# Ranking one head by itself, loading three U blocks with the query weights, and fetching late rows two ahead instead of four

## The chip, the cores and the metric

The kernel runs on one core of a Trainium2 chip. The metric is the device time of one execution in microseconds. Times are given for the whole program: the trunk layer with its caches and states, and the expert stage behind it.

## The reference

One inference step of one layer: 272 prompt rows (16 learned tokens and 256 new ones) and 8 × 8 rows of running sequences, 336 tokens of width 1024. The trunk (convolution branch, state-space branch, gates, output projection) is not touched by the change. Behind it stands a mixer that picks experts by product keys:

```python
q = (xb @ w_q).reshape(T, PEER_HEADS, 2, D_KEY // 2)
s = jnp.einsum('thcd,hckd->thck', q, keys).astype(jnp.float32)
s1, i1 = lax.top_k(s[:, :, 0], PEER_TOPK)
s2, i2 = lax.top_k(s[:, :, 1], PEER_TOPK)
cand = (s1[..., :, None] + s2[..., None, :]).reshape(T, PEER_HEADS, PEER_TOPK * PEER_TOPK)
sc, f = lax.top_k(cand, PEER_TOPK)
ids = (jnp.take_along_axis(i1, f // PEER_TOPK, axis=-1) * N_KEYS
       + jnp.take_along_axis(i2, f % PEER_TOPK, axis=-1))
g = jax.nn.softmax(sc, axis=-1)
act = jax.nn.gelu(jnp.einsum('thkd,td->thk', U[ids], xb).astype(jnp.float32), approximate=False)
w = (g * act).astype(xb.dtype)
return jnp.einsum('thk,thkd->td', w, V[ids])
```

There are 8 heads, 128 × 128 = 16384 experts with a row of U and a row of V each (1024 floats), and 16 experts for each token and head. Both outputs of the tokens are normalised behind it.

## The kernel before

Of the 320 tokens that reach the expert stage, 128 and another 16 are served by **gathering**: their chosen rows of U and V are fetched from memory. The other 176 are served **densely**: all U and V are streamed through TensorE (PE) and the unwanted experts are multiplied by zero.

**Queries and ranks.** Sixteen query projections (two per head; L1097 to L1113) are computed in program order. Each loads a block of weights (`weight`, L241: a load on SP into one of four raw buffers, a high part cast on ScalarE (ACT), a low part subtracted on GpSimd (POOL) or VectorE (DVE), two buffers each), makes 24 matmuls, copies the query to SBUF on ACT and multiplies it by the keys (psc, L1105). The scores are copied on ACT, for the gathered tokens into `sco` (9 buffers), for the dense ones into `sall`. `top16` (L995) finds the 16 best of 128 with five VectorE operations. `heads` (L1053) then ranks four heads of the gathered tokens: the sums of pairs, their 16 best, the table look-up of the ids, the ids in `gid`, and the softmax weights in `ggw`. It is called behind projections 7 and 15. The rank tasks of the dense tokens (`topk_tasks`, L1124) come later in program order; those of projections above 5 are ordered behind the first write of `gid`.

**Fetches.** A column is the n-th expert of all 128 gathered tokens, so one fetch (L1083) is an indirect DMA on POOL's queue of 128 rows of 8 KB, 1 MB, into one of five buffers `wuv` (one of which first holds a row of norm weights). There are 144: columns 0 to 63, 16 for the 16 extra tokens, 64 to 127. `ahead(n)` (L1092) gives out fetches up to n + 3. It is called once behind projection 7 and then by every `pick_row`. From the 93rd U block on, a fetch waits for the block matmul that lies `LEAD` = 4 blocks before the newest one in program order. `pick_row(n)` (L1212) is a dot product on VectorE (L1195), two small steps on ACT (L1197, L1198), and the weighted sum of V on VectorE (L1203).

**Dense blocks.** U and V have 128 blocks each of 512 KB, loaded on SP into a ring of eight buffers that served the weights before (`ring`, L1257). `u_block` (L1267) makes 16 matmuls into one of six PSUM buffers, and ACT writes the Gelu into S (L1274). S lies where the inputs of the query projections lay. `g_step` (L1280) multiplies S by the softmax weights of the chosen experts; its short matmuls `pg` (L1301) are ordered behind U or V blocks. `v_block` (L1363) makes 16 matmuls into standing sums. The transposes `pix` (L1163) that bring the dense ranks to PE are ordered behind U blocks 38 and 50.

**Order.** The program order interleaves tasks: `Feed` (L1239) spreads the rank tasks and 44 pick rows over the first 88 U blocks, 30 pick rows and half of the G steps over the other 40, 42 pick rows and the other half over the first 64 V blocks, and the last 29 of 145 rows over the rest. A scheduler then orders each engine's instructions from this program order, by its own estimate of the times; each engine works through its list in that order. Where `add_manual_dep` is used with `NoSync` only this order is bound.

The constants that matter: `HG` = 4 heads a call, `UV` = 5 buffers, `SB` = 88, `HB` = 64, `LASTP` = 126.

## Time and profile before

| | |
|---|---|
| runs | 1375.5, 1370.0, 1370.71 us; median 1370.71 |
| profiled execution | 1375.22 us, of which the span is 1373.5 |
| granted TensorE clock, mean | 0.983 |
| moved in all | 382.05 MB, mean 278 GB/s |
| fetches | queue q0: 20736 packets, 151.00 MB |
| loads and stores of SP | queue q1: 65056 packets, 227.46 MB |

The page is read from its slices: each stands for a fortieth of the span, 34.3 us. The trunk fills slices 0 to 15, the queries 16 and 17, the U blocks 18 to 28, the V blocks 29 to 39. Busy time, clock and transfer rate then show which stage is limited by what. An engine's idle time matters only where the chain of work that ends last passes through it; of that chain PE has 77%, DVE 12% and the transfers 8% of the span. The lines that carry this stand in the prediction.

### The profile page before, as it was taken

What the parts mean: (1) busy time and instruction counts of PE and PEld (TensorE: products, weight loads), DVE (VectorE), ACT (ScalarE), POOL (GpSimd) and SP (SyncE); (2) the same over time, 40 slices, a digit from 0 to 9 for tenths busy, and PEclk for the clock granted to TensorE, in tenths of its full rate; (3) what the DMA queues carried; (4) which work ended last, traced back from release to release, by engine and by line L of the source; (5) the groups of instructions that cost most, each with busy time, mean ns of one, the idle gap of its engine ahead of it and who ended that gap; (6) DMA issues with size and microseconds to landing.
All of it is one profiled execution on the core that took longest, in us unless ns stands there. A gap on an engine that the chain in (4) does not pass through costs nothing.

```text
span 1373.5 us, 24602 instructions
## 1 busy us (share of the span) xinstructions
PE 1319.4 (96%) x9324; PEld 1250.6 (91%) x9324; DVE 1017.6 (74%) x2340; ACT 526.4 (38%) x1393; POOL 581.7 (42%) x492
## 2 busy tenths in 40 slices
PE   9999999999999999998999988999999999987997
PEld 7888888888889999898998988999999999976897
DVE  7898777887866346799999885668787777766543
ACT  6777777777666434442222121111111111111101
POOL 2477776786746667542212331123222212344110
PEclk9999999999999999999999998999999999999999
DMA  6445545445344445439999999899999999999993
GB/s 237 160 127 171 166 160 162 142 149 187 108 142 127 150 154 165 148 114 380 398 413 393 409 416 362 288 416 363 372 416 415 380 377 390 395 417 416 414 412 113
DMA packets 87094, 382.05 MB, mean 278 GB/s; under 512 B 10144, under 2 KB 15648, under 8 KB 66368
## 3 DMA queue, kind: packets, MB, share of 16 engines
q1 hardware_dynamic: 65056, 227.46, 45.7%
q0 software_dynamic: 20736, 151.00, 27.3%
q10 hardware_dynamic: 1184, 2.02, 0.4%
q8 instruction: 73, 1.20, 0.3%
q14 instruction: 45, 0.37, 0.1%
HBM read 367.41 MB, written 13.03 MB: 277 GB/s over the span
## 4 chain that ended last, share of the span: by engine, by line
PE 77%; DVE 12%; DMA 8%; ACT 2%; issue 1%; POOL 0%; ACTq 0%; DVEq 0%
PE pj L150 30%; PE va L1366 19%; PE pj L1272 16%; DMA eraw<-in_vE_dram 5%; PE pg L1301 4%; PE pst L150 2%; DMA eraw<-in_uT_dram 2%; DVE wuv L1195 1%; DVE ygat L1203 1%; PE po L150 1%; PE py L150 1%; DVE pcv L473 1%; PE pdec L150 1%; PE ptr L155 1%; PE psc L1105 1%
## 5 line engine op out<-in xcount | busy, mean ns | idle before, releaser
L1083 POOL DMA_INDIRECT wuv<-in_peer_uv_dram,gid x144 | 183.0, 1271 | 523.4 <-DVE ygat L1203 159.7
L1272 PE MATMUL pj<-nd,eraw 128*128 128x176 f32 x2048 | 325.4, 320 | 11.5 <-DMA eraw<-in_uT_dram 7.6
L1366 PE MATMUL va<-S,eraw 128*128 128x176 f32 x2048 | 318.0, 315 | 18.9 <-DMA eraw<-in_vE_dram 18.9
L218 POOL TENSOR_TENSOR wl<-wraw,wh 128x1024 fp32r<-128x1024 f32 x111 | 267.2, 2408 | 149.7 <-ACT wh L217 78.0
L1366 PEld LDWEIGHTS va<-S,eraw 128*128 128x128 f32 x2048 | 307.6, 191 | 24.4 <-DMA eraw<-in_vE_dram 22.1
L1272 PEld LDWEIGHTS pj<-nd,eraw 128*128 128x128 f32 x2048 | 314.8, 195 | 13.5 <-ACT S L1274 8.8
L150 PE MATMUL pj<-ah,wh 128*128 128x336 f32 (+1 forms) x768 | 243.8, 329 | 0.7 <-ACT xnf L193 0.7
L150 PE MATMUL pj<-al,wh 128*128 128x336 f32 (+1 forms) x768 | 233.8, 318 | 0.0
L1203 DVE SCALAR_TENSOR_TENSOR ygat<-wuv,scg,ygat 128x1024 f32<-128x1024 f32 x128 | 163.9, 1280 | 57.8 <-ACT scg L1198 56.5
L1197 ACT ACTIVATE scg<-scg 128x1 f32<-128x1 f32 x144 | 29.0, 202 | 418.1 <-DVE wuv L1195 412.8
L1195 DVE SCALAR_TENSOR_TENSOR wuv<-wuv,x2m 128x1024 f32<-128x1024 f32 x128 | 156.0, 1218 | 42.6 <-DMA wuv<-in_peer_uv_dram,gid 42.6
L217 ACT CAST wh<-wraw 128x1024 fp32r<-128x1024 f32 x125 | 131.2, 1050 | 117.1 <-PE pj L150 79.9
L473 DVE SCALAR_TENSOR_TENSOR pcv<-ccat,vec,pcv 128x256 f32<-128x256 f32 x464 | 148.8, 379 | 17.1 <-ACT pcv L471 17.1
L150 PEld LDWEIGHTS pj<-ah,wh 128*128 128x128 f32 x768 | 147.1, 192 | 8.6 <-ACT xnf L193 2.7
L150 PEld LDWEIGHTS pj<-al,wh 128*128 128x128 f32 x768 | 146.5, 192 | 0.7
L150 PE MATMUL pj<-ah,wl 128*128 128x336 f32 (+1 forms) x768 | 137.0, 315 | 0.0
L150 PEld LDWEIGHTS pj<-ah,wl 128*128 128x128 f32 x768 | 120.5, 188 | 0.8 <-issue 0.7
L1274 ACT ACTIVATE S<-pj 128x176 f32<-128x176 f32 x128 | 37.6, 312 | 157.3 <-PE pj L1272 155.2
L1301 PE MATMUL pg<-oh 128*128 128x64 bf16 x1056 | 74.9, 242 | 0.0
L1308 DVE TENSOR_TENSOR S<-S,pg 128x192 f32<-128x192 f32 (+1 forms) x66 | 31.6, 506 | 56.9 <-PE pg L1301 56.9
L1301 PEld LDWEIGHTS <-oh 128*128 128x128 bf16 x1056 | 70.9, 117 | 2.2
L487 DVE SCALAR_TENSOR_TENSOR pj<-mcat,vec,pj 128x360 f32<-128x360 f32 x96 | 56.3, 588 | 3.6 <-ACT pj L485 3.6
(366 smaller groups left out, 1703.4 us busy)
## 6 DMA issues: line engine op xcount, KB each, us to landing
eraw<-in_uT_dram SPq DMA_DIRECT2D x128, 512.0 KB
eraw<-in_vE_dram SPq DMA_DIRECT2D x128, 512.0 KB
wraw<-in_w_in_dram SPq DMA_DIRECT2D x80, 512.0 KB
st<-in_state_dram SPq DMA_DIRECT2D x8, 1024.0 KB
out_ssm_s_dram<-st SPq DMA_DIRECT2D x8, 1024.0 KB
wraw<-in_w_mo_dram SPq DMA_DIRECT2D x16, 512.0 KB
wraw<-in_w_q_dram SPq DMA_DIRECT2D x16, 512.0 KB
wraw<-in_w_co_dram SPq DMA_DIRECT2D x8, 512.0 KB
```

Source lines behind the costliest of these rows:

```text
L150: i_ = nc.tensor.matmul(*a_, **kw)
L217: (nc.vector.tensor_copy if on_dve else nc.scalar.copy)(h, src)
L218: (nc.gpsimd if on_pool else nc.vector).tensor_tensor(l, src, h.bitcast(F32), op=OP.subtract)
L473: t = nc.vector.scalar_tensor_tensor(o, i_, wv, a_, op0=OP.mult, op1=OP.add)
L487: nc.vector.scalar_tensor_tensor(o, cat[:, w:w + n], wv, o, op0=OP.mult, op1=OP.add)
L1083: i_ = nc.gpsimd.indirect_dma_start(out=u, out_offset=None, in_=ia["peer_uv"], in_offset=bass.IndirectOffsetOnAxis(ap=gid[:, c:c + 1], axi ...
L1195: nc.vector.scalar_tensor_tensor(u[:, :D], u[:, :D], 1.0, x2m if c < NPICK else x2e, op0=OP.mult, op1=OP.mult, accum_out=w)
L1203: nc.vector.scalar_tensor_tensor(a_, u[:, D:], scg[:, c:c + 1], a_, op0=OP.mult, op1=OP.add)
L1272: i_ = nc.tensor.matmul(p[:, :ND], raw[:, k, :], nd[:, k, :], start=(k == 0), stop=(k == KD - 1))
L1274: nc.scalar.activation(Sv(b), p[:, :ND], AF.Gelu)
L1301: i_ = nc.tensor.matmul(pg[:, q, :], B[:, q // 4, :, q % 4], A[:, c_, q // 4, :, q % 4], start=(c_ == 0), stop=(c_ == 2))
L1366: i_ = nc.tensor.matmul(va[k // 2][:, k % 2], raw[:, k, :], Sv(b), start=False, stop=(b == 127), skip_group_check=True)
```

## The change

`heads` gets the number of heads as an argument. It is called for head 0 behind projection 1, for heads 1 to 3 behind projection 7, and for heads 4 to 7 behind projection 15. The first call of `ahead` stays behind projection 7 in program order, and fetches need only the ids of their own column. `ahead` gives out four fetches as before while at most 64 V blocks have been given out, and two afterwards (`DEEP`, `NEAR`).

Behind projection 6, U blocks 0 to 2 are loaded into a tile of their own (`pre`, 12 KB per partition). Their matmuls are taken out of `u_block` into `u_mm`, stand behind the sixteen projections in program order, and are ordered on PE behind the first score matmul of projection 12 (`PREJ`). `u_block` then only takes their Gelu. All other blocks are loaded and multiplied as before.

```diff
--- before.py
+++ after.py
@@ -43,6 +43,10 @@
 NCOL = NPICK + (NPICK // XQ if NX else 0)
 XAT = 64
 HG = 4
+BATCH = ((0, 1), (1, 3), (4, 4))
+NPRE = 3
+PREJ = 12
+FETCH = 7
 LEAD = 4
 GT = 8
 SB = 88
@@ -55,6 +59,8 @@
 RB = 4
 OH = 2
 UV = 5
+DEEP = 4
+NEAR = 2
 GLAG = 14
 PLACE = (38, 50)
 LASTP = 126
@@ -1050,28 +1056,28 @@
 
         early = []
 
-        def heads(h0):
-            hs_ = slice(h0, h0 + HG)
-            cs = slice(16 * h0, 16 * (h0 + HG))
-            sf = table(128, HG, si[0][:, 2 * h0:2 * h0 + 2 * HG])
-            c, cf = candidates(128, HG, sv[0].rearrange("p (h c) k -> p h c k", c=2)[:, hs_])
-            for h in range(HG):
+        def heads(h0, n_):
+            hs_ = slice(h0, h0 + n_)
+            cs = slice(16 * h0, 16 * (h0 + n_))
+            sf = table(128, n_, si[0][:, 2 * h0:2 * h0 + 2 * n_])
+            c, cf = candidates(128, n_, sv[0].rearrange("p (h c) k -> p h c k", c=2)[:, hs_])
+            for h in range(n_):
                 top16(cv0, ci0, cf[:, h], h0 + h)
-            ab = places(128, HG, ci0.rearrange("p h k -> p (h k)")[:, cs])
-            pk = kp.tile([128, 2, HG * 16], F32, name="pkh")
+            ab = places(128, n_, ci0.rearrange("p h k -> p (h k)")[:, cs])
+            pk = kp.tile([128, 2, HG * 16], F32, name="pkh")[:, :, :n_ * 16]
             for half in range(2):
-                look(pk[:, half], 128, HG, ab[half], sf, half, c)
-            idf = kp.tile([128, HG * 16], F32, name="idh")
+                look(pk[:, half], 128, n_, ab[half], sf, half, c)
+            idf = kp.tile([128, HG * 16], F32, name="idh")[:, :n_ * 16]
             nc.vector.scalar_tensor_tensor(idf, pk[:, 0], float(NK), pk[:, 1], op0=OP.mult, op1=OP.add)
             early.append(nc.vector.tensor_copy(gid[:, cs], idf).ins.name)
-            g_ = kp.tile([128, HG, 16], F32, name="gh")
-            nc.vector.tensor_tensor(g_, cv0[:, hs_], cv0[:, hs_, 0:1].to_broadcast([128, HG, 16]), op=OP.subtract)
+            g_ = kp.tile([128, HG, 16], F32, name="gh")[:, :n_]
+            nc.vector.tensor_tensor(g_, cv0[:, hs_], cv0[:, hs_, 0:1].to_broadcast([128, n_, 16]), op=OP.subtract)
             act(g_, g_, AF.Exp, scale=rsT[:, 0:1])
-            sm = kp.tile([128, HG], F32, name="smh")
+            sm = kp.tile([128, HG], F32, name="smh")[:, :n_]
             nc.vector.tensor_reduce(sm, g_, axis=AX.X, op=OP.add)
             nc.vector.reciprocal(sm, sm)
             nc.vector.tensor_tensor(ggw[:, cs].rearrange("p (h k) -> p h k", k=16), g_,
-                                    sm[:, :, None].to_broadcast([128, HG, 16]), op=OP.mult)
+                                    sm[:, :, None].to_broadcast([128, n_, 16]), op=OP.mult)
 
         COLS = list(range(XAT)) + list(range(NPICK, NCOL)) + list(range(XAT, NPICK))
         pend = {}
@@ -1090,10 +1096,26 @@
             return u
 
         def ahead(n):
-            for i_ in range(n, min(n + UV - 1, NCOL)):
+            for i_ in range(n, min(n + (DEEP if len(vstep) <= HB else NEAR), NCOL)):
                 if i_ not in pend:
                     pend[i_] = gather(COLS[i_])
 
+        def u_mm(b, raw):
+            tag, nb = (("pj", 3), ("y", 2), ("pj", 3), ("y", 2), ("pj", 3), ("pb", 1))[b % 6]
+            p = ps.tile([128, PJ], F32, name="pj", tag=tag, bufs=nb)[:, :T]
+            for k in range(KD):
+                i_ = nc.tensor.matmul(p[:, :ND], raw[:, k, :], nd[:, k, :], start=(k == 0), stop=(k == KD - 1))
+                if k == 0 and b < NPRE:
+                    tc.add_manual_dep(i_.ins, scored[PREJ], mybir.DependencyInfo(mybir.DependencyClass.NoSync,
+                                                                                 mybir.DependencyReason.DATA),
+                                      reason="behind the scores")
+            ustep.append(i_.ins.name)
+            return p
+
+        scored = []
+
+        us = ExitStack()
+        up = us.enter_context(tc.tile_pool(name="up", bufs=1))
         for j in range(16):
             w = weight(ia["w_q"], j)
             p = pj()
@@ -1102,15 +1124,24 @@
             nc.scalar.copy(qT[:, :T2], p[:, :T2])
             p = misc([128, 3, NK], "psc")
             for i, (t0, L) in enumerate(KTILES):
-                nc.tensor.matmul(p[:L, i], qT[:, t0:t0 + L], keys[:, j, :], start=True, stop=True)
+                i_ = nc.tensor.matmul(p[:L, i], qT[:, t0:t0 + L], keys[:, j, :], start=True, stop=True)
+                if i == 0:
+                    scored.append(i_.ins.name)
                 s_ = sall[:, i - 1, j] if i else kp.tile([128, NK], F32, name="sco", bufs=9)
                 nc.scalar.copy(s_[:L], p[:L, i])
                 if i == 0:
                     top16(sv[i], si[i], s_[:L], j)
-            if j % (2 * HG) == 2 * HG - 1:
-                heads(j // 2 - HG + 1)
-            if j == 2 * HG - 1:
+            for h0, n in BATCH:
+                if j == 2 * (h0 + n) - 1:
+                    heads(h0, n)
+            if j == FETCH:
                 ahead(0)
+            if j == 6:
+                pre = up.tile([128, NPRE, D], F32, name="pre")
+                for b in range(NPRE):
+                    nc.sync.dma_start(pre[:, b], ia["uT"][b])
+        early_u = [u_mm(b, pre[:, b].rearrange("p (k m) -> p k m", k=KD)) for b in range(NPRE)]
+        us.close()
         qs.close()
         xs.close()
         s0p = top.enter_context(tc.tile_pool(name="s0p", bufs=1, side=RIGHT))
@@ -1265,12 +1296,7 @@
             return raw.rearrange("p (k m) -> p k m", k=KD)
 
         def u_block(b):
-            raw = block(ia["uT"], b)
-            tag, nb = (("pj", 3), ("y", 2), ("pj", 3), ("y", 2), ("pj", 3), ("pb", 1))[b % 6]
-            p = ps.tile([128, PJ], F32, name="pj", tag=tag, bufs=nb)[:, :T]
-            for k in range(KD):
-                i_ = nc.tensor.matmul(p[:, :ND], raw[:, k, :], nd[:, k, :], start=(k == 0), stop=(k == KD - 1))
-            ustep.append(i_.ins.name)
+            p = early_u[b] if b < NPRE else u_mm(b, block(ia["uT"], b))
             nc.scalar.activation(Sv(b), p[:, :ND], AF.Gelu)
 
         def after(i_, name):
```

## The prediction

> **What bounds the kernel now.** The page comes first: its head, the engines, the forty slices.
>
> ```profile
> span 1373.5 us, 24602 instructions
> PE 1319.4 (96%) x9324; PEld 1250.6 (91%) x9324; DVE 1017.6 (74%) x2340; ACT 526.4 (38%) x1393; POOL 581.7 (42%) x492
> DMA  6445545445344445439999999899999999999993
> GB/s 237 160 127 171 166 160 162 142 149 187 108 142 127 150 154 165 148 114 380 398 413 393 409 416 362 288 416 363 372 416 415 380 377 390 395 417 416 414 412 113
> ```
>
> The matrix engine is busy nearly everywhere, and from slice 18 (about 620 us) the transfers run at some 415 GB/s too. So two resources are near their limits in the expert stage, which the change touches. The view of busy time by windows shows where PE falls behind. Columns: window, length, busy time (count) of PE, PEld, DVE, ACT, POOL; clock, DMA share, GB/s.
>
> ```profile
> 600.00:620.00 20.00, 20.00 (x134) 18.52 (x134) 19.57 (x90) 8.07 (x23) 9.57 (x4) 1.00 0.45 146
> 645.00:763.00 118.00, 113.52 (x725) 112.62 (x726) 117.19 (x389) 30.28 (x98) 28.92 (x23) 0.96 1.00 401
> 763.00:805.00 42.00, 42.00 (x296) 41.90 (x297) 34.16 (x51) 9.65 (x43) 16.18 (x12) 1.00 1.02 412
> 805.00:840.00 35.00, 27.41 (x194) 26.50 (x193) 21.33 (x34) 4.83 (x21) 7.26 (x6) 0.85 1.02 415
> 840.00:994.00 154.00, 154.00 (x1277) 153.01 (x1276) 113.68 (x179) 28.05 (x106) 34.76 (x27) 1.00 0.94 354
> 994.00:1193.00 199.00, 199.00 (x1626) 196.40 (x1625) 153.19 (x249) 22.06 (x86) 44.45 (x41) 1.00 1.00 395
> 1204.00:1282.00 78.00, 59.13 (x357) 54.45 (x356) 51.16 (x61) 9.95 (x40) 31.00 (x18) 0.98 1.02 416
> 1282.00:1345.00 63.00, 63.00 (x424) 63.00 (x424) 25.18 (x30) 4.97 (x20) 9.37 (x8) 1.00 1.01 406
> ```
>
> In 1282 to 1345 PE does 424 matmuls in 63 us, 6.73 per us, 2.38 us per block of 16: full speed. At that rate the 357 of 1204 to 1282 are 53 us of work, so **25 us are lost** there; the 725 of 645 to 763 are 108, so 10 are lost. For 805 to 840 the short G matmuls must be kept apart, with the same view of the U line alone:
>
> ```profile
> 800.00:840.00 40.00, 27.97 (x150) 26.47 (x151) 0.87 1.02 415
> 805.39 1.65 PE L1301 MATMUL pg<-oh 128*128 128x64 bf16 x24
> 806.86 5.03 PE L1272 MATMUL pj<-nd,eraw 128*128 128x176 f32 x32
> ```
>
> 150 U matmuls are 22.3 us; the three G groups in between (24 matmuls, 1.47 us from one start to the next) 4.4. So **13 us are lost** in 800 to 840. What ends both stalls is a block that has not landed, because row fetches take the bandwidth:
>
> ```profile
> 833.41 5.03 PE L1272 MATMUL pj<-nd,eraw 128*128 128x176 f32 x16 [3.91 <-DMA eraw<-in_uT_dram]
> 1228.25 2.65 PE L1366 MATMUL va<-S,eraw 128*128 128x176 f32 x16 [1.10 <-DMA eraw<-in_vE_dram]
> 1232.02 2.65 PE L1366 MATMUL va<-S,eraw 128*128 128x176 f32 x16 [1.12 <-DMA eraw<-in_vE_dram]
> q0 software_dynamic: 2283, 16.63, 67.1%
> q1 hardware_dynamic: 2286, 8.32, 34.4%
> ```
>
> The two q rows are the DMA view of 1205 to 1265. Packets are equal, bytes are two to one for the fetches, and a V block comes every 3.77 us (1228.25 to 1232.02), not every 2.38. The fetches come in bursts; POOL's windows for the fetch line alone (length, busy, count):
>
> ```profile
> 600.00:763.00 163.00, 34.76 (x29) 0.97 0.93 366
> 763.00:830.00 67.00, 23.02 (x18) 0.97 1.02 414
> 1193.00:1264.00 71.00, 33.12 (x21) 0.98 1.02 417
> 1264.00:1322.00 58.00, 11.81 (x11) 1.00 1.02 415
> ```
>
> Spacing is 3.7 us in 763 to 830, 3.4 in 1193 to 1264, above 5 in the other two: each burst has a stall in it. The first exists because until 763 VectorE is full of ranking; afterwards only picks are left in its order.
>
> **Part 1: head 0 alone, fetches and U blocks early.** The first ids exist when the cast to gid runs:
>
> ```profile
> 574.94 0.27 ACT L1107 COPY sco<-psc 128x128 f32<-128x128 f32 x1 [0.56 <-PE psc L1105]
> L1066 DVE CAST gid<-idh x2: 184/186/188, 622.5 to 693.7; 128x64 int32<-128x64 f32 x2
> 622.92 1.15 POOL L1083 DMA_INDIRECT wuv<-in_peer_uv_dram,gid  x1 [6.67 <-DVE sv L997]
> 632.86 1.21 DVE L1195 SCALAR_TENSOR_TENSOR wuv<-wuv,x2m 128x1024 f32<-128x1024 f32 x1
> 580.00:600.00 20.00, 17.39 (x115) 1.00 0.29 88
> 566.00:580.00 14.00, 7.96 (x36) 0.76 0.29 94
> ```
>
> (The last two are windows of VectorE.) Head 0 needs scores 0 and 1; the second is copied at 575, and VectorE still has idle time then, so its ids can exist near 590 to 600 and the first pick near 610 rather than 632.9: 20 us earlier, at some 5 us a pick four picks. Four fetches of 1.05 MB and three U blocks of 0.52 MB are 5.8 MB, 14 us of transfer at 415 GB/s, moved to a time when the engines are 0.29 to 0.45 busy. That is not the gain: in 645 to 763 VectorE is 117.19 of 118 us busy, so picks done earlier push ranking later. The gain is a shorter burst. With four of 18 picks gone, at about 3.8 us each while transfers limit, it ends 15 us sooner, of the 25 between 805 and 830; 60% of 13 us is 8. I take **7 us**, bounds 0 (VectorE hands out no pick earlier) and 13.
>
> The U blocks by themselves: 48 matmuls move between projections 13 to 15, but PE is 20.00 of 20 busy there, so nothing is saved; ahead of 645 six blocks can be computed in either order, for the six PSUM buffers. They are ordered behind score 12, and behind them on PE stand the last projections; their loads are some 40 us old by then, so PE waits for none. Three load issues move on SP ahead of the weights of projections 7 to 15, which have four raw buffers; bandwidth is free, so 0.
>
> The gap that follows:
>
> ```profile
> 644.24 0.44 PE L1105 MATMUL psc<-keys,qT 128*64 128x128 f32 x2 [2.72 <-ACT sall L1107]
> 643.50 0.20 ACT L1197 ACTIVATE scg<-scg 128x1 f32<-128x1 f32 x1 [2.53 <-DVE wuv L1195]
> 644.00:648.00 4.00, 2.76 (x9) 2.76 (x10) 0.57 1.01 417
> ```
>
> A score copy stood behind a pick's Gelu in ACT's order; PE ran dry and its clock fell to 0.57. Moved picks may dissolve this or put the same hold, and ACT's table changes between Exp and Gelu, elsewhere: bounds −10 (all of 645 to 763) and +10, taken **−2**.
>
> Cost: ranking in three calls, not two, adds 26 VectorE instructions (one table, two candidate sums, five places, twelve look-ups, six for ids and softmax). At 0.19 us (the cast's row) that is 5 us, against 8.7 idle in 566 to 600. Some meet POOL's low-part subtractions:
>
> ```profile
> L1073 DVE TENSOR_TENSOR ggw<-gh,smh x2: 217/1272/2328, 614.0 to 684.6; 128x64 f32<-128x64 f32 x2
> 613.85 2.40 POOL L218 TENSOR_TENSOR wl<-wraw,wh 128x1024 fp32r<-128x1024 f32 x1 [2.37 <-ACT sall L1107]
> ```
>
> The same product takes 0.217 us alone and 2.328 beside a POOL subtraction, ending with it. The Trainium skill, "GPSIMD Engine Reference", "Key points", says GpSimd shares its SBUF interfaces with VectorE, so that VectorE instructions with two SBUF inputs contend. The trace agrees by these two numbers; it speaks against ranking earlier, among the subtractions. By the rows alone: two more such meetings, 2.1 us each, 4 at most. Between 0 (idle time covers all) and +9 I take **+1**, near the idle row.
>
> **Part 2: two ahead from the 65th V block on.** A fetch is tied to the V block four before the newest at the moment when it is given out. The last 29 of the 145 pick rows are spread over 61 blocks, 2.1 blocks each; given out two rows later, a fetch waits 4.2 blocks longer. In the burst a block comes every 3.77 instead of 2.38 us, with one fetch, and the fetches gain 1 − 1/2.1 = 0.52 columns a block on their ties. A lead smaller by two ends the burst 2/0.52 = 3.8 blocks sooner: 3.8 × 1.39 = **5 us**. Bounds: 0 (the same bytes must still pass) and 12 (half of the 25). The tail is covered:
>
> ```profile
> 1320.75 1.90 POOL L1083 DMA_INDIRECT wuv<-in_peer_uv_dram,gid  x1 [3.83 <-PE va L1366]
> 1332.25 1.28 DVE L1203 SCALAR_TENSOR_TENSOR ygat<-wuv,scg,ygat 128x1024 f32<-128x1024 f32 x1 [0.60 <-ACT scg L1198]
> 1346.53 0.43 DVE L1345 COPY wraw<-ygat 128x512 f32<-128x512 f32 x1 [12.99 <-PE va L1366]
> ```
>
> The last sum would move 10 us, from 1333.5 to 1344, and the finish waits for PE until 1346.5 anyway. Without that cover each us late adds a us to this output only, which is not the last.
>
> **Sum.** −7 − 2 + 1 − 5 = −13 us. The profiled execution took 1375.22 us, 1.7 outside its span, and becomes 1362; it stands 4.5 above the median of the runs, 1370.71 (1370.0 to 1375.5). So **1358**.
>
> **Rivals.** *VectorE is the wall:* picks keep their place in its order, early fetches sit in the five buffers, the burst stays. For it: 117.19 of 118 us. Against: the first pick did wait for its rows until 632. It leaves −5 + 1, so 1367.
>
> *Depth does nothing late.* Equal packets mean one outstanding fetch takes as much as four; if fetches never wait on their ties, Part 2 gives 0: 1363. The Trainium skill states this share as a rule ("DMA: Bandwidth & Descriptors", "Queues, rings and completion order": each DMA engine goes round the queues packet by packet). By that rule, the 2283 and 2286 packets agree. Against 0 speak the 11 fetches after 1264, at a spacing of 5.3 us; the row of the last names PE's V matmul as what it waited for.
>
> *Slower: a fetch in POOL's order holds a low part.* Fetch 6 needs the buffer that pick 0 frees; today it follows the last subtraction:
>
> ```profile
> 640.13 0.94 POOL L1083 DMA_INDIRECT wuv<-in_peer_uv_dram,gid  x1 [11.08 <-DVE si L1005]
> 620.99 0.75 PE L150 MATMUL pj<-ah,wl 128*128 128x320 f32 x4
> ```
>
> Tomorrow it may stand between subtractions of projections 10 to 15. The last low part is ready at 613.85 + 2.40 = 616.25 and used at 620.99: 4.7 us of slack. It decides where a wait exceeds that. An 11 us wait leaves 6.3 us of dry PE and a clock at 0.57 behind it, 1.7 us in the 4 of the row above: 8 each. Two or three such are 16 to 24, less the 5 of Part 2 and some of Part 1: about +12, so 1383.
>
> **How the numbers follow.** Forecast 0.53 (its own range 1349 to 1365), VectorE wall 0.23, depth 0.08, slower 0.16. Half a per cent, 6.9 us, is what a measurement can tell from no change: faster is below 1363.9, slower above 1377.6. Faster: the forecast but a tail of 0.03, half of depth, 0.04 of the wall: 0.58. Same: the wall's rest, half of depth, the tail and a mild hold of 0.02: 0.28. Slower 0.14. The range reaches from 1348 to 1375; beyond it lie the worse holds and the far end of the bounds.
>
> **What would show it.** Right: gid first cast near 595, first pick near 610, spacing above 4 us after 763, fewer lost microseconds in 800 to 840; the late burst ends about four blocks sooner; last fetch some 10 us nearer the end. Wrong: 18 fetches again after the ranking (the wall); POOL waits in front of L218 above 4.7 us, with a clock below 1.00 before 640 (the hold); matrix waits for the picks' transposes at U block 50, because ranking ends later than 763.

## The result, and the profile after

The changed kernel takes **1379.48 us** (median of five runs, 1378.86 to 1381.03), the kernel before in the same measurement 1370.71 us (five runs, 1367.81 to 1375.5). The ratio is 1.0064, with a 95% interval of 1.0047 to 1.0081: slower by some 9 us, where 13 us faster were forecast. The profiled execution took 1379.09 us, 1.8 of them outside its span. That is 0.4 below the median, while the profiled execution of the kernel before stands 4.5 above its own (and those of three runs below, "before, two ahead", "no split" and "fetches behind low parts", 4.2 to 4.3 above theirs), so stages of two profiles can differ by some us for that reason alone.

The page of the changed kernel, head, engines and the transfer rate by slices:

```profile
span 1377.3 us, 24625 instructions
PE 1317.3 (96%) x9324; PEld 1246.0 (90%) x9324; DVE 1025.6 (74%) x2366; ACT 530.4 (39%) x1396; POOL 589.3 (43%) x492
GB/s 236 161 128 168 169 157 171 137 151 181 114 152 123 152 147 178 187 246 319 309 347 414 388 399 414 245 417 384 333 415 414 390 365 377 403 417 416 413 415 145
```

VectorE has its 26 instructions more. The transfers begin a slice earlier (246 GB/s in slice 17, before 114), as they were meant to, but run at 319, 309 and 347 in the three slices behind, where the kernel before moved 380 to 413. The same stretches as in the prediction, in the view of busy time by windows:

```profile
600.00:620.00 20.00, 13.55 (x78) 11.89 (x76) 18.57 (x63) 6.17 (x19) 14.48 (x10) 0.83 0.95 370
645.00:763.00 118.00, 108.01 (x693) 104.77 (x692) 115.52 (x433) 30.47 (x96) 26.38 (x21) 0.97 0.92 357
763.00:805.00 42.00, 35.15 (x221) 34.51 (x220) 38.99 (x89) 11.28 (x37) 13.32 (x9) 0.92 0.98 380
805.00:840.00 35.00, 35.00 (x272) 34.82 (x271) 22.82 (x34) 7.31 (x29) 11.85 (x8) 1.00 1.02 414
1204.00:1282.00 78.00, 63.13 (x400) 59.39 (x399) 49.32 (x60) 9.45 (x38) 30.52 (x18) 1.00 1.02 416
1282.00:1345.00 63.00, 61.39 (x406) 60.20 (x405) 30.84 (x39) 6.46 (x26) 11.17 (x10) 1.00 1.02 414
```

Two of the forecast signs are there. The stall of 805 to 840 is gone (35.00 busy, before 27.41); whether the early picks removed it is taken up with the experiments. In 1204 to 1282 PE makes 400 matmuls in place of 357, and gives back a part of that in 1282 to 1345 (406 in place of 424). The loss stands ahead of them: in 600 to 620, where PE was busy without a gap before, it now works 13.55 of 20 us, at a clock of 0.83.

How much each stage takes is read from the first start and the last start of a group. First the kernel before, then the changed one: the Gelus that write S, one for each U block, and the V matmuls.

```profile
L1274 ACT ACTIVATE S<-pj x128: 297/317/327, 644.9 to 994.1; 128x176 f32<-128x176 f32 x128
L1366 PE MATMUL va<-S,eraw x2048: 312/313/567, 996.3 to 1362.8; 128*128 128x176 f32 x187
```

```profile
L1300 ACT ACTIVATE S<-pj x128: 296/317/365, 655.9 to 1000.5; 128x176 f32<-128x176 f32 x128
L1392 PE MATMUL va<-S,eraw x2048: 312/313/418, 1002.7 to 1365.8; 128*128 128x176 f32 x187
```

The first Gelu on S comes 11.0 us later. From there to the first V matmul, called the U stage below, it is 346.8 us in place of 351.4, and the V matmuls, the V stage, take 363.1 in place of 366.5. So in these two profiles two stages gained 4.6 and 3.4 us, and the query projections lost 11. That leaves 3 us, where the medians differ by 8.8: part of the two gains belongs to that one execution of before. What happened in the projections, in order of time:

```profile
590.12 2.38 POOL L224 TENSOR_TENSOR wl<-wraw,wh 128x1024 fp32r<-128x1024 f32 x1 [1.89 <-ACT qT L1124]
...
598.97 1.15 POOL L1089 DMA_INDIRECT wuv<-in_peer_uv_dram,gid  x1 [6.47 <-DVE sall L1009]
...
604.15 0.94 POOL L1089 DMA_INDIRECT wuv<-in_peer_uv_dram,gid  x1 [0.30 <-issue]
604.99 5.88 DVE L1226 SCALAR_TENSOR_TENSOR wuv<-wuv,x2m 128x1024 f32<-128x1024 f32 x1 [1.44 <-DMA wuv<-in_peer_uv_dram,gid]
605.12 4.66 POOL L224 TENSOR_TENSOR wl<-wraw,wh 128x1024 fp32r<-128x1024 f32 x2
607.52 1.44 PE L156 MATMUL pj<-ah,wl 128*128 128x320 f32 x8 [2.56 <-POOL wl L224]
610.91 0.20 ACT L1228 ACTIVATE scg<-scg 128x1 f32<-128x1 f32 x1 [9.44 <-DVE wuv L1226]
612.59 0.80 PE L1127 MATMUL psc<-keys,qT 128*128 128x128 f32 x2 [3.63 <-ACT sco L1131]
...
696.62 0.94 POOL L1089 DMA_INDIRECT wuv<-in_peer_uv_dram,gid  x1 [21.74 <-DVE cv L1003]
...
779.34 0.36 PE L1194 MATMUL pix<-cst,pick 64*128 64x64 f32 x1 [6.85 <-DVE pick L1055]
```

The view is the timeline: start, duration, engine and line, tiles, and in brackets the idle time before with what ended it. GpSimd waits 6.47 us for head 0's ids with a low part queued behind the fetch; then it issues five fetches, another 6 us, and the next two low parts run only at 605.12. PE waits for the first of them at 607.52. Beside these two subtractions the first pick's product takes 5.88 us (1.21 by itself); its Gelu stands in ScalarE's queue and waits 9.44 us for it, with a weight cast and score copies behind; PE waits for a score copy at 612.59. Later there is a hole of 21.74 us in the fetches, until the ids of heads 1 to 3 exist, and a wait of 6.85 us for the picks' transposes, which the dense tokens' ranking has ready at 779, before at 763.

The trace shows these waits. It doesn't show which of them makes the others, and three things changed in the same stretch: a ranking call more, fetches in another place of GpSimd's queue, and picks and an Exp in another place of ScalarE's.

### The profile page after: what moved, and what is told of

Same layout as the page of the kernel before. It is cut to its first block, busy times and chain, and to the rows that moved or that the text cites. A ratio compares the mean times of both kernels' runs of the same rounds, so it can differ in the third digit from the quotient of the medians.

```text
span 1377.3 us, 24625 instructions
## 1 busy us (share of the span) xinstructions
PE 1317.3 (96%) x9324; PEld 1246.0 (90%) x9324; DVE 1025.6 (74%) x2366; ACT 530.4 (39%) x1396; POOL 589.3 (43%) x492
## 4 chain that ended last, share of the span: by engine, by line
PE 80%; DVE 11%; DMA 6%; ACT 2%; issue 0%; POOL 0%; ACTq 0%; DVEq 0%
PE pj L156 31%; PE va L1392 19%; PE pj L1107 17%; DMA eraw<-in_vE_dram 5%; PE pg L1327 5%; DVE wuv L1226 2%; PE pst L156 2%; DVE ygat L1234 2%; PE po L156 1%; PE py L156 1%; PE pdec L156 1%; ACT L199 1%; PE ptr L161 1%; DMA wdt<-in_w_dt_dram 1%; PE pq L156 1%; PE psc L1127 1%
## 5 line engine op out<-in xcount | busy, mean ns | idle before, releaser
L1089 POOL DMA_INDIRECT wuv<-in_peer_uv_dram,gid x144 | 189.5, 1316 | 537.0 <-PE va L1392 127.0
L1107 PE MATMUL pj<-nd,eraw 128*128 128x176 f32 x2000 | 313.9, 317 | 6.3 <-DMA eraw<-in_uT_dram 4.3
L1107 PEld LDWEIGHTS pj<-nd,eraw 128*128 128x128 f32 x2000 | 303.3, 193 | 8.8 <-ACT S L1300 4.3
L1226 DVE SCALAR_TENSOR_TENSOR wuv<-wuv,x2m 128x1024 f32<-128x1024 f32 x128 | 162.8, 1272 | 58.2 <-DMA wuv<-in_peer_uv_dram,gid 58.2
```

Of the source, the lines that this page charges most:

```text
L1089: i_ = nc.gpsimd.indirect_dma_start(out=u, out_offset=None, in_=ia["peer_uv"], in_offset=bass.IndirectOffsetOnAxis(ap=gid[:, c:c + 1], axi ...
L1107: i_ = nc.tensor.matmul(p[:, :ND], raw[:, k, :], nd[:, k, :], start=(k == 0), stop=(k == KD - 1))
L1226: nc.vector.scalar_tensor_tensor(u[:, :D], u[:, :D], 1.0, x2m if c < NPICK else x2e, op0=OP.mult, op1=OP.mult, accum_out=w)
```

## The experiments

All medians in one table, each with its ratio to the kernel before on the same chip. "S" is the first Gelu on S, "V" the first and last start of a V matmul, in the profiled execution.

| kernel | median us | ratio, 95% interval | S | V |
|---|---|---|---|---|
| changed | 1379.48 | 1.0064 (1.0047 to 1.0081) | 655.9 | 1002.7 to 1365.8 |
| four ahead again | 1386.14 | 1.0117 (1.0097 to 1.0136) | 657.0 | 1006.3 to 1373.2 |
| before, two ahead | 1366.07 | 0.9961 (0.9946 to 0.9975) | 646.3 | 994.9 to 1358.0 |
| no split | 1363.63 | 0.9942 (0.9929 to 0.9955) | 645.3 | 992.8 to 1355.4 |
| no U blocks ahead | 1379.05 | 1.0056 (1.0043 to 1.0069) | 656.2 | 1007.2 to 1367.1 |
| before, U blocks ahead | 1368.46 | 0.9992 (0.9981 to 1.0002) | 644.0 | 990.1 to 1355.1 |
| fetches behind low parts | 1372.87 | 1.0012 (1.0003 to 1.0022) | 654.1 | 1003.9 to 1364.0 |
| Gelus behind score copies | 1382.90 | 1.0084 (1.0066 to 1.0102) | 658.4 | 1008.0 to 1370.3 |
| fetches, Gelus, Exps behind | 1374.46 | 1.0024 (1.0014 to 1.0035) | 644.3 | 1000.6 to 1363.8 |
| Gelus, Exps behind | 1381.39 | 1.0076 (1.0063 to 1.0089) | 645.4 | 1005.6 to 1366.7 |
| fetches, later Exps behind | 1373.54 | 1.0026 (1.0016 to 1.0037) | 654.4 | 1000.2 to 1361.9 |
| fetches, later Exps, Gelus behind | 1375.56 | 1.0039 (1.0026 to 1.0052) | 644.2 | 1000.5 to 1363.5 |
| gate | 1378.61 | 1.0054 (1.0034 to 1.0074) | 658.1 | 1006.9 to 1365.5 |
| gate, fetches behind | 1373.08 | 1.0011 (0.9997 to 1.0026) | 654.3 | 998.9 to 1360.9 |
| no split, spare call early | 1373.89 | 1.0026 (1.0015 to 1.0037) | 652.4 | 999.3 to 1362.1 |
| no split, spare call late | 1365.55 | 0.9963 (0.9950 to 0.9975) | 643.2 | 991.7 to 1353.9 |

### The late part, alone and taken away

```diff
-NEAR = 2
+NEAR = 4
```

> The changed kernel with the late columns fetched four ahead again; the ranking, the early fetches and the three U blocks stay. The changed kernel's V stage, first V matmul to last, was 363.1 us against 366.5 before. Theory (the loss is all in the query projections, and two ahead gives a little back): the V stage goes back to about 366.5 and the median to 1383 us (1381 to 1385). Rival A (the late part does nothing, the 3.4 us came from elsewhere): V stage 363, median 1379.5. Rival B (two ahead itself costs time): median below 1377.

```diff
 def ahead(n):
-    for i_ in range(n, min(n + UV - 1, NCOL)):
+    for i_ in range(n, min(n + (UV - 1 if len(vstep) <= HB else 2), NCOL)):
```

> The kernel before with only the late columns fetched two ahead. Theory (the late part gains about what the V stages differ by): V stage 363 to 364 us in place of 366.5, last fetch some 10 us later than 1320.8, median 1367 us (1365 to 1369). Rival A (it does nothing): 1370.7 within 1. Rival B (it costs time): above 1372.

With four ahead the V matmuls take 366.9 us again, and the median rises by 6.7 us, more than was expected (the V matmuls of the two profiles differ by 3.8 us); this profile also reaches its first V matmul 3.6 us later. Alone, two ahead gains 4.9 us and its V matmuls take 363.1. The rows of that run, the V matmuls and the last of the fetches:

```profile
L1366 PE MATMUL va<-S,eraw x2048: 312/313/417, 994.9 to 1358.0; 128*128 128x176 f32 x187
L1083 POOL DMA_INDIRECT wuv<-in_peer_uv_dram,gid x144: 935/1147/3064, 624.2 to 1325.4; - x144
```

The last fetch starts 32.6 us ahead of the last V matmul; before it was 42.0 (1362.8 less 1320.8). Both rivals fall, and the late part isn't where the time was lost.

### Which part of the first half

```diff
-BATCH = ((0, 1), (1, 3), (4, 4))
+BATCH = ((0, 4), (4, 4))
```

> The changed kernel with heads 0 to 3 ranked together again, in two calls of four; the three U blocks loaded ahead and two ahead stay. Theory (the split of the first ranking is the whole loss, and the U blocks are worth nothing): the median is that of two ahead alone, 1366 us (1364 to 1368), PE's busy time in 600 to 620 is 20 of 20 and in 640 to 660 near 16.4. Rival (the U blocks cost time): 1370 us or more. Rival (the U blocks fill the stall near 644): 1362 or less.

```diff
-NPRE = 3
+NPRE = 0
...
-                pre = up.tile([128, NPRE, D], F32, name="pre")
```

> The changed kernel without the three U blocks loaded ahead; head 0 alone, the early fetches and two ahead stay. Theory (the U blocks are worth nothing): 1379.5 us (1377 to 1382), PE's busy time in 600 to 620 near 13.5 of 20 again. Rival (the U blocks fill part of the holds, since they are work that needs neither a score nor a pick): 1383 us or more. Rival (their loads and their place cost time): 1376 or less.

```diff
-BATCH = ((0, 1), (1, 3), (4, 4))
+BATCH = ((0, 4), (4, 4))
...
-NEAR = 2
+NEAR = 4
```

> The kernel before with only the three U blocks loaded ahead: heads in two calls of four, four ahead throughout. Theory (U blocks worth 0 to 2.4 us, by the two pairs so far): 1368.5 to 1371 us. Rival (they gain more with four ahead): below 1368.

Without the split the kernel takes 1363.63 us, 15.9 less than the changed one and less than the kernel before. It is the best of all that were run, 0.4 below the range of its theory. Its windows show the queries as they were before:

```profile
600.00:620.00 20.00, 20.00 (x134) 18.70 (x134) 19.14 (x90) 8.04 (x24) 9.56 (x4) 1.00 0.43 133
620.00:640.00 20.00, 20.00 (x134) 18.53 (x132) 19.76 (x105) 5.24 (x18) 5.67 (x6) 1.00 0.89 348
640.00:660.00 20.00, 17.25 (x92) 16.02 (x92) 20.00 (x84) 5.62 (x24) 5.81 (x5) 0.83 0.91 334
```

The U blocks are worth 0 to 2.4 us: 2.1 alone, with an interval that reaches 1; 2.4 beside two ahead (1366.07 less 1363.63, from two measurements); nothing in the changed kernel. So **ranking head 0 alone**, with what follows from it in the queues, **is the whole loss**, and it costs 16 us.

One more thing is in these rows. The U stage takes 347.5 us without the split and 346.8 with it, less than before (351.4) in both, so the early picks have hardly a part in it. It is the U blocks that shorten it: without them the changed kernel has 351.0 (its V stage is 3.2 us shorter then, 359.9, and the median shows nothing).

Nor did the early picks remove the stall of 805 to 840. First the kernel before with the U blocks alone, where no head is ranked early, then the split with the fetches behind the low parts (the next section):

```profile
767.37 0.36 PE L1194 MATMUL pix<-cst,pick 64*128 64x64 f32 x1 [7.25 <-DVE pick L1055]
805.00:840.00 35.00, 35.00 (x304) 34.60 (x303) 26.07 (x42) 6.73 (x26) 9.07 (x7) 1.00 1.02 414
```

```profile
805.00:840.00 35.00, 28.22 (x222) 26.70 (x222) 28.92 (x41) 6.81 (x29) 10.27 (x10) 1.00 1.02 416
```

With the U blocks PE reaches the place of the transposes before the ranking is done, waits 7.25 us there, and finds no stall behind it. With the split, and a wait of only 0.8 us at the transposes, the stall is back. In every profile of this case a wait of 3 us or more at the transposes leaves less than 2 us of the stall; that the loads catch up during that wait fits this, but was not tested.

### The order on GpSimd and on ScalarE

Every fetch is bound behind the last low part in GpSimd's order (`lows` collects the subtractions, `FETCH` only moves the call behind projection 15 in program order):

```diff
+            tc.add_manual_dep(i_.ins, lows[-1], mybir.DependencyInfo(mybir.DependencyClass.NoSync,
+                mybir.DependencyReason.DATA), reason="behind the low parts")
             steps = ustep[SB:] + vstep
```

> The changed kernel with every fetch ordered behind the last low part on GpSimd; the ranking of head 0 alone, the three U blocks and two ahead stay, and the picks' Gelus may still stand among the score copies. Theory 'order on GpSimd': GpSimd's 6.5 us wait ahead of a low part goes, no pick's product runs beside a subtraction (the first takes near 1.2 us, not 5.88), PE's busy time in 600 to 620 rises from 13.55 to 19 or more of 20, median 1370 to 1374 us. Theory 'order on ScalarE': score copies still wait for Gelus, later; the U stage starts 4 to 8 us late and the median is 1375 to 1379. Rival 'late ranking': 1378 to 1381.

The picks' Gelus are bound behind the last score copy in ScalarE's order instead:

```diff
-            nc.scalar.activation(w, w, AF.Gelu)
+            i_ = nc.scalar.activation(w, w, AF.Gelu)
+            tc.add_manual_dep(i_.ins, copied[-1], mybir.DependencyInfo(mybir.DependencyClass.NoSync,
+                mybir.DependencyReason.DATA), reason="behind the scores")
```

> The changed kernel with every pick's Gelu ordered behind the last score copy on ScalarE; head 0 is still ranked alone and five fetches still stand in GpSimd's order ahead of the last low parts. Theory 'order on ScalarE' (the wh casts and score copies of the last projections wait for Gelus of picks, 29.6 us of waits in 590 to 665): these waits go, PE's busy time in 600 to 620 rises from 13.55 to 17 or more of 20, the first Gelu on S comes near 649 in place of 655.9, median near 1373 us (1371 to 1376). Rival 'order on GpSimd' (the fetch that waits 6.5 us for the ids, ahead of the low parts, is what costs): PE still lacks some 6 us in 600 to 620, median 1378 to 1381. Rival 'late ranking' (heads 1 to 3 ranked late): gid's second cast still near 696, median 1378 to 1381.

The fetches are worth **6.6 us** (1379.48 less 1372.87). PE works 17.86 of 20 us in 600 to 620, less than was expected, and loses 5.1 in 620 to 640. In this run the first fetch follows the last low part, at 617.78, and another instruction holds ScalarE, the Exp of heads 1 to 3:

```profile
624.59 0.33 ACT L199 ACTIVATE gh<-gh,rsT 128x48 f32<-128x48 f32 x1 [10.00 <-DVE ci L1015]
625.13 1.42 PE L1133 MATMUL psc<-keys,qT 128*128 128x128 f32 x4 [7.26 <-ACT sco L1137]
```

Moving the Gelus alone made it 3.4 us slower, against the theory that named ScalarE's order. In its trace the same Exp now waits 13 us:

```profile
640.77 0.33 ACT L199 ACTIVATE gh<-gh,rsT 128x48 f32<-128x48 f32 x1 [13.11 <-DVE gh L1074]
641.31 0.79 PE L1127 MATMUL psc<-keys,qT 128*128 128x128 f32 x2 [9.54 <-ACT sall L1131]
```

That Exp is not the reason for most of it: with it moved as well the kernel takes 1381.39 us, 1.5 less (the second run below). Both kinds were moved: the Exps of `heads` in a function of their own behind the loop, each behind the last score copy, once with and once without the order of the fetches.

```diff
-            g_ = kp.tile([128, HG, 16], F32, name="gh")[:, :n_]
+            soft0.append(lambda: norm(h0, n_, hs_, cs))
...
+        def norm(h0, n_, hs_, cs):
...
+            tc.add_manual_dep(i_.ins, copied[-1], mybir.DependencyInfo(mybir.DependencyClass.NoSync,
+                mybir.DependencyReason.DATA), reason="behind the scores")
```

> The changed kernel with three orders written out: every fetch behind the last low part on GpSimd, and the picks' Gelus and the Exps of the early heads behind the last score copy on ScalarE. Head 0 is still ranked alone. Theory (what costs is that instructions that wait for ranking stand in in-order queues ahead of the projections' work): no wait of a score copy or wh cast above 3 us in 598 to 650, PE lacks 4 us or less in 600 to 660 (before: 3.6), and the median is that of two ahead alone, 1364 to 1369 us. Rival 'late ranking' (one head ahead makes the other ids and the dense tokens late, whatever the queues do): second cast to gid later than 693.7, PE waits for the picks' transposes after 763, median 1372 or more.

> The same with only the two orders on ScalarE (picks' Gelus and the early heads' Exps behind the last score copy); five fetches stand ahead of the last low parts on GpSimd, as in the changed kernel. Theory (both queues hold): PE waits 2 to 3 us for a low part near 607 and runs on a lower clock behind it, median 2 to 6 us above the run with all three orders. Rival 'ScalarE alone': within 1.5 us of it. Rival 'late ranking': both at 1378 or more.

The holds go: the first Gelu on S comes at 644.3, and PE lacks 2.9 us in 600 to 660. But the median is 1374.46, where the rival of late ranking had 1372 or more (its other sign, a wait for the transposes behind 763, is not there). The time comes back in the U stage, which takes 356.3 us from the first Gelu on S. With Gelus and Exps so late the picks end late, and the fetches stop:

```profile
620.00:640.00 20.00, 20.00 (x133) 18.33 (x131) 20.00 (x124) 4.13 (x15) 2.13 (x3) 1.00 0.94 380
640.00:660.00 20.00, 17.10 (x100) 16.30 (x100) 20.00 (x116) 5.68 (x23) 0.00 (x0) 0.91 0.54 161
661.89 0.94 POOL L1100 DMA_INDIRECT wuv<-in_peer_uv_dram,gid  x1 [39.15 <-DVE ygat L1251]
```

GpSimd issues nothing in 640 to 660 and the transfers fall to 161 GB/s. The sixth fetch, at 661.89, has waited 39.15 us, and the trace names a pick's weighted sum on VectorE as what released it, the instruction that frees a buffer; no run tested it. The pair of runs does give the price of the fetches a second time: 1381.39 less 1374.46 is **6.9 us**, beside the 6.6 above and 0.9 above the range of its theory.

### What is left with the fetches behind

Some 9 us are left between 1372.87 and 1363.63. First the Exps of the later heads alone, then these and the Gelus; head 0's Exp stays early in both.

```diff
-            act(g_, g_, AF.Exp, scale=rsT[:, 0:1])
+            i_ = act(g_, g_, AF.Exp, scale=rsT[:, 0:1])
...
+            if h0:
+                tc.add_manual_dep(i_.ins, copied[-1], mybir.DependencyInfo(mybir.DependencyClass.NoSync,
+                    mybir.DependencyReason.DATA), reason="behind the scores")
```

> Head 0 ranked alone, every fetch behind the last low part on GpSimd, and of ScalarE's orders only one: the Exps of heads 1 to 3 and 4 to 7 behind the last score copy; head 0's Exp and the picks' Gelus stay where the planner puts them. It differs from the run with fetches behind the low parts (1372.87 us) in that Exp alone, which waited 10.0 us for VectorE at 624.6 in front of score copies. Theory (the rest of the loss of the split is that Exp): the wait goes, PE is busy 19 or more of 20 in 600 to 620 and 620 to 640, the first Gelu on S comes at 645 to 649 in place of 654.1, median 1364 to 1368 us. Rival (the split makes ranking late, whatever stands in the queues): the first Gelu on S early, the U stage 5 us or more longer than 350, median 1371 or more.

> As the run with only the Exps behind, and the picks' Gelus behind the last score copy as well; head 0's Exp stays early. Theory: no score copy waits for VectorE, the first Gelu on S comes at 644 to 646, but the first picks' sums and with them the buffers for the sixth fetch come later than 650, so the gain is lost again in the U stage: median 1367 to 1373 us, not below the run with only the Exps behind. Rival (order on ScalarE is all that counts): 1 to 3 us below that run.

No theory had both numbers. With the Exps alone the median is the rival's (1371 or more), but S starts at 654.4, late as before, where both wanted it early. With the Exp out of the way, the next instruction of ScalarE's queue that needs VectorE waits as long:

```profile
635.50 0.20 ACT L1247 ACTIVATE scg<-scg 128x1 f32<-128x1 f32 x1 [10.42 <-DVE wuv L1245]
636.23 0.69 PE L1144 MATMUL psc<-keys,qT 128*64 128x128 f32 x2 [6.32 <-ACT sall L1148]
```

So the wait of 10 us belongs to no single instruction of ScalarE: VectorE is late. With the Gelus moved too, S starts at 644.2, as expected, and the U stage pays again, 356.3 us; the median, 1375.56, is above the range of the theory.

One reason for a late VectorE could be the gate of the dense tokens' ranking. It waits for the first write of `gid`; since the split that is head 0's, and the dense ranks come in ahead of heads 1 to 3.

```diff
-                tc.add_manual_dep(i_.ins, early[0], mybir.DependencyInfo(mybir.DependencyClass.NoSync,
+                tc.add_manual_dep(i_.ins, early[1], mybir.DependencyInfo(mybir.DependencyClass.NoSync,
```

> The changed kernel with one line back in its old meaning: the ranking of the dense tokens' scores from the seventh on waits for the ids of heads 1 to 3 (in the kernel before: for those of heads 0 to 3; in the changed kernel: for head 0's alone). Fetches still stand ahead of the last low parts. Theory 'two causes' (fetches ahead of low parts, and dense ranking let in ahead of heads 1 to 3): the hold at 605 to 612 stays, but the cast of heads 1 to 3 comes well before 696, the gap in the fetches from 674 to 696 goes, and the median falls to 1369 to 1375 us. Rival (order on GpSimd and the split itself are all, the gate nothing): 1378 to 1381.

> Both: the dense ranking behind the ids of heads 1 to 3, and every fetch behind the last low part; head 0 still ranked alone, three calls, three U blocks, two ahead. Theory 'two causes': what is left is the cost of the third call alone, PE is busy 19 or more of 20 in 600 to 620 and 620 to 640, the first Gelu on S comes at 644 to 648, VectorE's 10 us wait on ScalarE's queue is 4 us or less, and the median is 1364 to 1368 us, against 1363.63 without the split. Rival (the third call fills VectorE by itself): first Gelu on S at 652 or later, median 1370 or more.

The gate is nothing: 1378.61 beside 1379.48, and 1373.08 beside 1372.87. The edit did what it was meant to do: in the first run the ids of heads 1 to 3 exist at 663.5, in the changed kernel at 696.2, in the second at 628.4, and at 657.5 in the run with only the fetches behind the low parts. Ids 29 to 33 us earlier are worth nothing. A hole in the fetches stays (24.25 us ahead of 688.69), but it is another one: those ids have long been there, and the trace names a pick's weighted sum as what released the fetch. The numbers of the second run are those of its rival, that the third call fills VectorE by itself. With the gate back, the Exp of heads 1 to 3 still waits, 5 us earlier:

```profile
619.28 0.34 ACT L199 ACTIVATE gh<-gh,rsT 128x48 f32<-128x48 f32 x1 [9.16 <-DVE gh L1078]
```

### The third call by itself

What remains is the call. It was put into the kernel without the split, into spare tiles that nothing reads, once behind projection 1 and once behind the ids of heads 0 to 3. The output doesn't depend on it, and fetches, picks and score copies keep the places in program order that they have without the split.

```diff
+        spare = (kp.tile([128, 1, 16], F32, name="cvx"), kp.tile([128, 1, 16], U32, name="cix"),
+                 kp.tile([128, 16], I32, name="gix"), kp.tile([128, 16], F32, name="ggx"))
...
-        def heads(h0, n_):
+        def heads(h0, n_, cv0, ci0, gid, ggw, real=True):
...
+            if j == 1:
+                heads(0, 1, *spare, real=False)
```

> The kernel without the split (heads in two calls of four, three U blocks, two ahead: 1363.63 us) with one ranking call of head 0 more behind query projection 1, into spare tiles that nothing reads; no fetch, pick or score copy changes its place. It is the third call by itself, beside the low parts. Theory (VectorE and GpSimd hold each other up: each two-input instruction of the call that meets a subtraction takes about 2 us in place of 0.2, five or six of them, and VectorE is then late for everything behind it): some five instructions of the call at 1.5 to 2.4 us, VectorE full in 580 to 600, a wait of 5 us or more for VectorE on ScalarE ahead of score copies or a later ranking, median 1370 to 1374 us. Rival (the call's work is small; what costs are the places of fetches, picks and Exps): 1363 to 1366.

> The same spare call, started behind the ids of heads 0 to 3 (about 623 us), where GpSimd has no subtraction left. Theory (the meetings with the subtractions are most of its price): its instructions at 0.1 to 0.35 us each, median 1364 to 1368 us, at least 4 below the run with the call early. Rival (VectorE's time is full there too, so the instructions count and not the meetings): within 2 us of that run.

Early, the call that nobody reads costs **10.3 us** (1373.89 less 1363.63, from two measurements). Late, it costs 1.9. It was bound behind the ids of heads 0 to 3, at 621, and ran at 694 to 708, where VectorE is nearly full too (13.25 of 14 us busy). The rival falls: the work is the same, so 8.3 us, from one measurement, are the price of its place. The early run, VectorE's two-input instructions that took more than 1.2 us and, ahead of three of them, the subtraction beside which they ran; behind the first, the Exp and the matmul that waited for it:

```profile
580.26 2.34 POOL L224 TENSOR_TENSOR wl<-wraw,wh 128x1024 fp32r<-128x1024 f32 x1 [7.47 <-PE pj L156]
580.63 2.00 DVE L1079 TENSOR_TENSOR gh<-cvx 128x16 f32<-128x16 f32 x1
582.66 0.31 ACT L199 ACTIVATE gh<-gh,rsT 128x16 f32<-128x16 f32 x1 [3.08 <-DVE gh L1079]
583.18 0.85 PE L1132 MATMUL psc<-keys,qT 128*128 128x128 f32 x4 [3.05 <-ACT sco L1136]
590.51 2.40 POOL L224 TENSOR_TENSOR wl<-wraw,wh 128x1024 fp32r<-128x1024 f32 x1 [7.91 <-PE pj L156]
590.94 2.12 DVE L1051 TENSOR_TENSOR cand<-cand,sf 128x256 bf16<-128x256 bf16 x1
...
595.13 2.10 DVE L1054 TENSOR_TENSOR cand<-cand 128x64 bf16<-128x64 bf16 x1
599.56 2.40 POOL L224 TENSOR_TENSOR wl<-wraw,wh 128x1024 fp32r<-128x1024 f32 x1 [2.38 <-ACT sall L1136]
599.79 2.19 DVE L1074 SCALAR_TENSOR_TENSOR idh<-pkh 128x16 f32<-128x16 f32 x1
...
609.46 2.06 DVE L1024 TENSOR_TENSOR cand<-sv 128x480 f32<-128x480 f32 x1
620.37 2.80 DVE L1048 TENSOR_TENSOR cand<-pab,iorep 128x1024 bf16<-128x1024 bf16 x1
```

The late run, the same instructions where GpSimd subtracts no more:

```profile
697.75 0.16 DVE L1082 TENSOR_TENSOR gh<-cvx 128x16 f32<-128x16 f32 x1
...
701.42 0.28 DVE L1054 TENSOR_TENSOR cand<-cand,sf 128x256 bf16<-128x256 bf16 x1
...
705.88 0.18 DVE L1077 SCALAR_TENSOR_TENSOR idh<-pkh 128x16 f32<-128x16 f32 x1
```

A product of 128x256 takes 0.28 us by itself and 2.12 beside a subtraction; sixteen columns take 0.16 or 0.18, and 2.00 or 2.19. Each of the first four ends within 0.2 us of the end of its subtraction (580.63 + 2.00 = 582.63, 580.26 + 2.34 = 582.60). Four of the call's own instructions lose 1.8 to 2.0 us each, 7.6 in all; the two last rows are the call of heads 0 to 3, pushed among the last subtractions, and lose about 1.5 and 2.1 more. That call loses 3.4 in the late run too, at other instructions (1.50 and 2.32 us), and half a us at a third. So VectorE loses some 7 us more in the early run, and its busy time over the whole execution says the same (1029.3 and 1022.3 us, 2374 instructions in each); 8.3 is the difference in time. How it gets to PE is seen in the early run's ScalarE: the call's own Exp waits 3.08 us for the first of the four, with a score copy behind it, and PE stands for 3.05 us; the Exp of heads 0 to 3 waits 4.97 us at 618.89, a pick's Gelu 5.25 at 639.60, and S starts at 652.4 in place of 643.2. That the meetings make the difference, and not the early place as such, is read from these rows: no run has the early call without the subtractions beside it.

## Why the prediction was wrong

**What held.** Head 0's ids came at 598.5 (forecast near 595) and the first pick at 605 (610). Two ahead was sized at 5 us and is worth 4.9 alone, 4.8 beside the U blocks (1368.46 less 1363.63) and 6.7 in the changed kernel; the last fetch came 9.5 us nearer to the last V matmul (10).

**What came true for another reason.** The stall of 805 to 840 vanished, but it vanishes with the U blocks alone as well, and stays in a run with the split, so it was no sign of a shorter burst: that was luck. The U blocks were costed at 0 and gave 0 to 2.4, with waits moved about in the U stage that the forecast did not have. The late burst was to end about four blocks sooner. It did not: with two ahead alone PE waits more than 0.5 us for a V block 15 times, the last at 1296, 16.2 us in all; in the kernel before 17 times, the last at 1282, 18.9 us. The waits get fewer and not earlier. The V stages of the profiles give 2.4 to 3.8 of the 5 us; where the rest arises stays open.

**The step that failed is the cost of the third call**: "two more such meetings, 2.1 us each, 4 at most", taken at +1 with a bound of +9. The size of a meeting was right (1.8 to 2.0 us lost each), and the prediction itself had said that it speaks against ranking earlier; the count was wrong. The call was counted by its 26 instructions against the idle time of 566 to 600. But from 590 to 613 of the early run a subtraction starts every 4.3 to 4.8 us, and in the rows above the next product or sum of two tensors ends only with it (two more, at 603.85 and 612.91, fell among searches for the best scores and held nothing). The call spreads over 22 us (580 to 602) and met all four subtractions in that time, and what it pushed back met two more. Measured: +10.3, just beyond the bound. The split's own call did the same: with the fetches behind the low parts it met five between 583 and 604 and lost 8.7 us, and the split costs 9.2 there (1372.87 less 1363.63). In the changed kernel it met three, 4.8 us lost, because the first fetch then held the subtractions back.

**The slower rival was true as well**, at a chance of 0.16: a fetch did hold a low part on GpSimd, for 6.47 us, above the 4.7 from which it was to decide. It was not the sixth fetch with its buffer, as the prediction had it (that one waited 4.25 us at 614, below 4.7), but the first, waiting for the ids that the stretched call delivered late; the five issues behind it held the low part for 6 us more, a term that the prediction did not have. One such hold was priced at 8 us; it measured 6.6 and 6.9. What this price is made of was not taken apart: fetches ahead of the low parts also bring the picks' products beside them (5.88 us), and both go with one edit.

**The gain of part 1** was sized at 7 us by the picks that leave the burst. Nearly nothing of it is due to them. With the call's ids used early and the fetches behind the low parts the kernel takes 1372.87; with the call's ids thrown away it takes 1373.89. That is 1.0 us for the early ids, within the spread of these runs, and even this is not theirs for certain: the thrown-away call has eight instructions more than the split adds (2374 beside 2366), and the 3.05 us for which PE stands at its Exp, where the split's Exp waits for nothing. "VectorE is the wall" had said so. Its reason, that VectorE is full until 763 and does later for ranking what it does earlier for picks, fits the transposes, ready at 779 in place of 763, but no run tested it. The wait of 6.85 us for them is no proof: without the split PE waits 7.25 at the same place. **The gap** at 644, sized at −2, moved with the queries: PE lacks 5.7 us in 640 to 660 (14.29 busy), before 3.6.

Along one path of kernels the loss adds up: −7.6 for two ahead and the U blocks (1363.63 beside 1371.23 in its measurement), +10.3 for the third call among the subtractions, −1.0 for its early ids, +6.6 for the fetches ahead of the low parts: +8.3. These are differences along the path, so their sum is the end less the start by construction; that the change itself measured 8.8 only says that the kernel before differed by 0.5 in the two measurements. Set against the forecast, the third call was 9.3 us dearer, the hold 6.6 that the sum did not have, part 1 some 6 short, the 2 of the gap did not come, and two ahead with the U blocks 2.6 better.

**What stays open** is why the U stage takes 356 us where all waits of ScalarE were moved behind the score copies. The hole in the transfers (161 GB/s) stands there, but no run took it away by itself. Open too is the price of the early call without the meetings.

## What to carry to other kernels

Where two engines hold each other up, count the meetings by the other engine's instructions that fall into the stretch, not by one's own that might be hit; that is the upper bound. A small chain spread over four subtractions met all four. A sign that comes true is worth checking in a run without the part that was to cause it: the stall of 805 to 840 also went where nothing was ranked early. When a wait goes away and the next instruction in the queue waits as long, the engine waited for is late; stop moving the waiters, and put the suspected work in by itself, read by nobody, in two places. A part of a change that gains (two ahead, here) can hide behind one that loses: undo each part alone before judging the whole.

## What was not expected of the hardware

The row of before showed a product of two tensors held beside a subtraction. That a cast with a single tensor input is held as well was not expected. In the run with fetches behind low parts a cast took 2.19 us at 615.64 (0.40 in the changed kernel, where it meets none), beside a subtraction of 615.21 to 617.61:

```profile
615.21 2.40 POOL L226 TENSOR_TENSOR wl<-wraw,wh 128x1024 fp32r<-128x1024 f32 x1 [2.36 <-ACT wh L225]
615.64 2.19 DVE L1035 CAST sf<-si 128x384 bf16<-128x384 uint32 x1
```

The other way round, a subtraction that meets a product of 1024 columns is stretched itself: two took 6.51 us together at 615.32 in the changed kernel, where one takes 2.40 by itself. The Trainium skill, "SBUF — State Buffer", "SBUF: two separate sides", describes the pair of ports that VectorE and GpSimd share as an exclusive lock that the first to start holds for its whole instruction, while the other fully blocks. The trace agrees with the full block: the first product of the changed kernel, 1.21 us by itself, took 5.88 beside two subtractions of 4.66 together, which is the sum of both. It does not settle who holds the lock: that product is recorded 0.13 us ahead of the first subtraction and ends behind the second.
